# Masked softmax on one core: the first tile's 6-row store is cut into 2 and 4 rows

## The chip, the cores and the metric

The kernel runs on one core of one Trainium2 chip. The metric is the device time of one execution in microseconds. A core has compute engines that work beside each other, each with its own list of instructions: TensorE (PE in the profile), VectorE (DVE), ScalarE (ACT), GpSimd (POOL) and SyncE (SP), which here only issues transfers. They wait for each other by semaphores. Transfers between the chip's memory and the core's on-chip buffer are carried out by 16 transfer (DMA) engines, which take their work from queues: q1 holds what SyncE issues, q0 what GpSimd issues.

## The reference

For each of 16 batches, a softmax along the last axis is taken over the first `length` columns; the columns behind stay zero.

```python
def reference(x, lengths):                    # x: 16 x 8 x 256 x 256 float32
    result = np.zeros_like(x)
    for b in range(batch):
        length = lengths[b]                   # 128 to 255
        masked = x[b, :, :, :length].copy()
        masked = masked - np.max(masked, axis=-1, keepdims=True)
        exp_masked = np.exp(masked)
        result[b, :, :, :length] = exp_masked / np.sum(exp_masked, axis=-1, keepdims=True)
    return result
```

The lengths of the draw are 188, 233, 229, 243, 195, 252, 165, 210, 222, 180, 209, 157, 159, 199, 214 and 248.

## The kernel before

One batch is one tile: 8 x 256 = 2048 rows of 256 columns, laid out as 128 partitions with 16 rows each, so that a partition's share of a tile is 16 KB in one piece in memory. `xt` has 8 slots of a tile; the tile at position n uses slot n modulo 8, and every step works in place. Positions 0, 1 and 2 hold batches 1, 2 and 3, position 3 holds batch 15, positions 4 to 14 the batches of that number, and position 15 holds batch 0 (`batch_of`). "Tile n" below means position n.

The order of work is written out by hand, with a list and semaphores for each engine.

- *Loads.* SyncE loads tile 0 in two halves (L137). GpSimd loads tiles 1 and 2 whole (L185) and all later ones through `pick` (L157), which branches on the batch's length and loads only as many columns as are needed, in steps of 8 from 160 to 240, or all 256; what a load leaves out was zeroed once by `fill` (L180). A load cut off in this way consists of short runs, a full one of 16 KB per partition. In the loop (L193) the load of tile n waits until the load of tile n - 2 has landed (L199) and until the slot's former tile n - 8 has been stored (L200). So about two loads are under way at a time.
- *Compute.* VectorE clips each tile from column 128 on (L241), which puts very low values behind the length; ScalarE takes the exponential row by row with the row's sum (L348), 16 instructions a tile; VectorE then takes the reciprocals of a half tile's 8 sums (L262) and multiplies the half by them (L265). On VectorE the clip of tile b + 1 stands between the two divisions of tile b, except for tile 1.
- *Stores.* SyncE's list (L138 to L148) goes through the tiles and, in each tile, through the pieces that `parts` gives. Each piece waits at L141 for the division of the half that it ends in. The first piece of each tile from tile 2 on waits at L145 until the tile two before has wholly landed. In tile 0 the piece that starts at row 2 also waits at L143 for `s_min` to reach 3, that is, for the clip of tile 1.
- *Semaphores of the stores.* Even and odd tiles have one each, `s_st[0]` and `s_st[1]`. A tile adds 64 in all, whatever its pieces, and both start at 64.
- *End.* After the last tile VectorE looks at the sums (L297 to L308) to see whether the plain path was good enough; if it was, nothing more is computed, and SyncE waits for the last store.

The pieces of a tile are given by `cuts`, in rows per partition:

```python
        if b == 0:
            cuts = [0, 2, half, nt]              # nt = 16, half = 8, quarter = 4
        elif b < 8:
            cuts = [0, half, half + quarter, nt]
```

Tiles 8 to 12 and 15 go out in two halves, 13 and 14 in one piece.

Of the kernel before, what the change touches and what calls it, by code (L numbers as in the profile page):

```python
# [21 lines left out]
def kernel(  # L22
# [12 lines left out]
    nt = rows // P  # L35
    half = nt // 2
    quarter = nt // 4
# [11 lines left out]
    def batch_of(pos):  # L49
        return pos + 1 if pos < ahead else {ahead: 15, 15: 0}.get(pos, pos)  # L50
# [7 lines left out]
    def parts(b):  # L58


        if b == 0:
            cuts = [0, 2, half, nt]
        elif b < 8:
            cuts = [0, half, half + quarter, nt]
        elif b < 13 or b == batch - 1:
            cuts = [0, half, nt]
        else:
            cuts = [0, nt]
        return [slice(i, j) for i, j in zip(cuts, cuts[1:])]
# [30 lines left out]
    with tc.tile_critical(no_gpsimd_drain=True):  # L100
# [34 lines left out]
        for h in range(2):  # L135
            s = slice(h * half, (h + 1) * half)
            nc.sync.dma_start(out=xt[:, 0, s], in_=x_f[batch_of(0), :, s]).then_inc(s_ld[h], 16)  # L137
        for b in range(batch):  # L138
            s_b = s_st[b % 2]
            for s in parts(b):  # L140
                nc.sync.wait_ge(s_out, 2 * b + (s.stop - 1) // half + 1)  # L141
                if b == 0 and s.start == 2:
                    nc.sync.wait_ge(s_min, 3)  # L143
                if b >= 2 and s.start == 0:
                    nc.sync.wait_ge(s_b, 64 * (b // 2 + 1))  # L145
                nc.sync.dma_start(  # L146
                    out=out_f[batch_of(b), :, s, :], in_=xt[:, b % slots, s, :]
                ).then_inc(s_b, 16 * max(1, (s.stop - s.start) // quarter))  # L148
        nc.sync.wait_ge(s_st[0], 64 * (batch // 2 + 1))


# [41 lines left out]
        with nc.Fori(0, batch // 2 - 2, 1, engines=[POOL]) as q:  # L193
            for par in range(2):
                n = 2 * q + (ahead + 1 + par)
                b = n % 15 if par == 1 else n
# [215 lines left out]
```

## Time and profile before

| | |
|---|---|
| median of 3 runs | 155.60 us (155.55, 155.60, 156.01) |
| the profiled execution | 155.76 us, of which 154.0 us from the first to the last instruction |
| busy: VectorE / ScalarE / GpSimd / TensorE | 117.0 / 105.3 / 22.6 / 0.3 us |
| moved | 61.57 MB, mean 400 GB/s |
| read from memory / written to it | 27.98 MB / 33.55 MB |
| transfers issued by SyncE for stores | 38 |

How to read it: the profile shows one execution. "Busy" counts an engine's own work, not its waiting and not the issuing of transfers. The strip of 40 slices gives the busy share of each fortieth of the span in tenths, 9 for 90% or more. A row of the timeline has start and duration in us, engine, line of the kernel, operation and tiles; "SPq" and "POOLq" are the sequencers of SyncE and GpSimd. In the queue view a row gives packets, MB, and the time that the packets took as a share of 16 transfer engines over the stretch looked at. In the table by stretches, each row gives the stretch, its length, the busy time of each engine with the number of its instructions, the granted clock, the busy share of the transfer engines and the GB/s. The chain of waits follows back from the last instruction of a compute engine through what released each step.

### The profile page before, as it was taken

How to read it: one execution, taken by the hardware profiler on the slowest of the kernel's cores; microseconds unless marked ns; L12 is line 12 of the kernel's file. 1: busy time of each engine (PE TensorE's matmuls, PEld its weight loads, DVE VectorE, ACT ScalarE, POOL GpSimd, SP SyncE). 2: the span in 40 equal slices, each digit the busy share in tenths (PEclk: the TensorE clock that was granted, in tenths of full speed). 3: DMA queues.
4: the chain of work that ended last, by engine and by line, in shares of the span. 5: the costliest groups of instructions: out<-in, count | busy, mean ns of one | idle time of the engine just before them, and what ended most of it. 6: DMA issues, size and time to landing. Idle time of an engine off the chain costs nothing.

```text
span 154.0 us, 1308 instructions
## 1 busy us (share of the span) xinstructions
PE 0.3 (0%) x2; PEld 0.2 (0%) x2; DVE 117.0 (76%) x91; ACT 105.3 (68%) x514; POOL 22.6 (15%) x30
## 2 busy tenths in 40 slices
PE   0000000000000000000000000000000000000000
PEld 0000000000000000000000000000000000000000
DVE  1349899988969696969698796969696566596820
ACT  3097799579595959596886949595959709639300
POOL 4893000102030200202020030211020000000000
DMA  4999999999999999999999999999999999999992
GB/s 102 424 449 430 420 358 387 425 432 427 410 400 386 422 408 422 411 412 417 400 419 414 408 418 403 415 418 412 414 425 418 424 408 419 420 445 434 415 424 100
DMA packets 10501, 61.57 MB, mean 400 GB/s; under 512 B 882, under 2 KB 994, under 8 KB 6914
## 3 DMA queue, kind: packets, MB, share of 16 engines
q1 hardware_dynamic: 5760, 35.65, 56.5%
q0 software_dynamic: 4736, 25.89, 41.7%
q14 instruction: 3, 0.02, 0.0%
q10 hardware_dynamic: 2, 0.00, 0.0%
HBM read 27.98 MB, written 33.55 MB: 400 GB/s over the span
## 4 chain that ended last, share of the span: by engine, by line
DMA 65%; DVE 17%; ACT 5%; issue 5%; ACTq 1%; POOLq 1%; POOL 1%; SPq 1%; PE 0%
DMA xt<-in_x_dram 43%; DMA out_dram<-xt 21%; DVE xt L265 9%; DVE xt L241 6%; ACT xt L348 5%; ACTq L348 1%; POOL xt L180 1%; DMA word<-in_lengths_dram 1%; DVE inv_sum L262 1%; SPq L146 1%; DVE ends L297 0%; POOLq L127 0%; POOLq L162 0%; POOLq L157 0%; DVE bad L300 0%
## 5 line engine op out<-in xcount | busy, mean ns | idle before, releaser
L348 ACT ACTIVATE xt<-xt (+1 forms) x256 | 102.4, 401 | 36.7 <-DVE xt L241 36.7
L265 DVE TENSOR_TENSOR xt<-xt,inv_sum 128x2048 f32<-128x2048 f32 x32 | 73.3, 2291 | 1.1
L348 ACT ACTIVATION_READ_ACCUMULATOR xt<-xt (+1 forms) x256 | 47.8, 187 | 0.0
L241 DVE SCALAR_TENSOR_TENSOR xt<-down,len_s,xt 128x2048 f32<-128x2048 f32 (+1 forms) x17 | 37.8, 2222 | 10.9 <-DMA xt<-in_x_dram 10.7
L157 POOL DMA_DIRECT2D xt<-in_x_dram x13 | 13.8, 1060 | 90.3 <-DMA out_dram<-xt 56.6
L262 DVE RECIPROCAL inv_sum<-row_sum 128x8 f32<-128x8 f32 x32 | 6.3, 198 | 16.0 <-ACT xt L348 16.0
L180 POOL MEMSET xt<- 128x1536 f32 x5 | 6.7, 1399 | 1.1 <-DVE len_s L232 1.1
L341 ACT ACT_TABLE_LOAD x1 | 1.3, 1283 | 1.6 <-SPq L100 1.6
L224 DVE TENSOR_SCALAR down<-iota_i 128x256 f32<-128x256 int32 x1 | 0.3, 299 | 1.6 <-POOL iota_i L170 1.6
L185 POOL DMA_DIRECT2D xt<-in_x_dram x2 | 1.2, 620 | 0.0
L297 DVE TENSOR_REDUCE ends<-row_sum 128x1 f32<-128x256 f32 x2 | 0.7, 408 | 0.0
L211 PE MATMUL count<-bad,ones_c 128*1 128x3 bf16 x1 | 0.2, 165 | 144.5 <-DVE bad L300 144.5
L229 DVE CAST len_b<-word 1x16 bf16<-1x16 int32 x1 | 0.2, 163 | 0.4 <-DMA word<-in_lengths_dram 0.4
L232 DVE TENSOR_SCALAR len_s<-len_f 128x16 f32<-128x16 f32 x1 | 0.2, 175 | 0.4 <-PE len_f L209 0.4
L170 POOL IOTA iota_i<- 128x256 int32 x1 | 0.3, 331 | 0.6 <-SPq L100 0.6
L308 DVE TENSOR_REDUCE redo<-count 1x1 f32<-1x3 f32 x1 | 0.1, 149 | 0.3 <-PE count L211 0.3
L300 DVE TENSOR_SCALAR bad<-ends 128x1 bf16<-128x1 f32 x3 | 0.3, 150 | 0.0
L211 PEld LDWEIGHTS count<-bad,ones_c 128*1 128x1 bf16 x1 | 0.1, 79 | 144.6 <-DVE bad L300 144.6
L176 POOL MEMSET seed<- 1x1 f32 x2 | 0.2, 226 | 0.0
L341 ACT ACTIVATE warm<-const-float32-0.0 128x1 f32<-128x1 f32 x1 | 0.2, 202 | 0.0
L173 POOL MEMSET ones<- 1x128 bf16 x1 | 0.2, 194 | 0.0
L209 PE MATMUL len_f<-len_b,ones 1*128 1x16 bf16 x1 | 0.2, 167 | 2.6 <-DVE len_b L229 2.6
(8 smaller groups left out, 0.8 us busy)
## 6 DMA issues: line engine op xcount, KB each, us to landing
out_dram<-xt SPq DMA_DIRECT2D x20, 1024.0 KB
xt<-in_x_dram POOLq DMA_DIRECT2D x4, 2048.0 KB, 14.7
out_dram<-xt SPq DMA_DIRECT2D x14, 512.0 KB
xt<-in_x_dram POOLq DMA_DIRECT2D x3, 1728.0 KB, 16.9
out_dram<-xt SPq DMA_DIRECT2D x2, 2048.0 KB
xt<-in_x_dram POOLq DMA_DIRECT2D x2, 1600.0 KB, 18.9
xt<-in_x_dram POOLq DMA_DIRECT2D x2, 1280.0 KB, 13.9
xt<-in_x_dram SPq DMA_DIRECT2D x2, 1024.0 KB, 6.6
```

The costliest lines, as they stand in the source:

```text
L146: nc.sync.dma_start(out=out_f[batch_of(b), :, s, :], in_=xt[:, b % slots, s, :]).then_inc(s_b, 16 * max(1, (s.stop - s.start) // quarter))
L157: nc.gpsimd.dma_start(out=xt[:, slot, :, :w], in_=x_n[:, b, :, :w]).then_inc(s_sw[par], 16)
L170: nc.gpsimd.iota(iota_i, pattern=[[1, seq_k]], base=0, channel_multiplier=0).then_inc(s_iota, 1)
L180: nc.gpsimd.memset(xt[:, b, :, low:], 0.0).then_inc(s_fill, 1)
L185: nc.gpsimd.dma_start(out=xt[:, b], in_=x_f[batch_of(b)]).then_inc(s_ld[b + 1], 16)
L211: nc.tensor.matmul(count, lhsT=ones_c, rhs=bad, start=True, stop=True).then_inc(s_count, 1)
L241: return nc.vector.scalar_tensor_tensor(out=t, in0=down[:, None, lo:hi].to_broadcast([P, s.stop - s.start, hi - lo]), scalar=len_s[:, batc ...
L262: step(nc.vector.reciprocal(out=inv_sum[:, b, s], in_=row_sum[:, b, s]))
L265: nc.vector.tensor_tensor(out=t, in0=t, in1=inv_sum[:, b, s, None].to_broadcast([P, half, seq_k]), op=ALU.mult,).then_inc(s_out, 1)
L297: step(nc.vector.tensor_reduce(out=ends[:, k : k + 1], in_=values, op=op, axis=AX))
L341: nc.scalar.activation(out=warm, in_=nc.const_aps.tensor(0.0, (P, 1), F32), func=EXP)
L348: ins = nc.scalar.activation(out=e, in_=e, func=EXP, accum_out=sum_h[:, i, j])
```

## The change

For the first tile, the piece from row 2 to row 8 is cut at row 4. The tile goes out as rows 0 to 2, 2 to 4, 4 to 8 and 8 to 16 of each partition: 256, 256, 512 and 1024 KB instead of 256, 768 and 1024 KB. Its four pieces add 16 each to `s_st[0]`, 64 in all as before; before, the three added 16, 16 and 32. All other tiles have the same pieces and the same increments as before. The waits at L141, L143 and L145 are unchanged; the one at L143 now stands ahead of the piece of rows 2 to 4.

```diff
         if b == 0:
-            cuts = [0, 2, half, nt]
+            cuts = [0, 2, quarter, half, nt]
         elif b < 8:
             cuts = [0, half, half + quarter, nt]
...
                 nc.sync.dma_start(
                     out=out_f[batch_of(b), :, s, :], in_=xt[:, b % slots, s, :]
-                ).then_inc(s_b, 16 * max(1, (s.stop - s.start) // quarter))
+                ).then_inc(s_b, 16 * (1 if b == 0 else (s.stop - s.start) // quarter))
```

In the order of instructions only SyncE's list changes: it has one transfer more, the others' lists are the same.

## The prediction

> **What bounds the kernel now.** I read the page first: the span, the busy shares, the strip of 40 slices, the queues. Then the chain of waits, SyncE's waits at the end, and a table by stretches.
>
> ```profile
> span 154.0 us, 1308 instructions
> PE 0.3 (0%) x2; PEld 0.2 (0%) x2; DVE 117.0 (76%) x91; ACT 105.3 (68%) x514; POOL 22.6 (15%) x30
> DMA  4999999999999999999999999999999999999992
> DMA packets 10501, 61.57 MB, mean 400 GB/s; under 512 B 882, under 2 KB 994, under 8 KB 6914
> q1 hardware_dynamic: 5760, 35.65, 56.5%
> q0 software_dynamic: 4736, 25.89, 41.7%
> ```
>
> No compute engine is over 76%, while the transfer engines stand at 9 from the second slice to the second last. Queue q1 holds the first tile's two loads and all 38 stores, each of 128 data packets and 16 tiny ones: 40 x 144 = 5760. Queue q0 holds the other loads.
>
> The chain of waits seems to say something else:
>
> ```profile
> 134.56 2.36 DVE xt L241
> 143.94 2.29 DVE xt L265
> 147.53 0.15 DVE redo L308
> ```
>
> It follows the last load through the last tile's compute, but it stops at the last engine instruction, at 147.7. SyncE, whose sequencer the chain does not end on, then still waits for stores:
>
> ```profile
> SPq L407 <- DMA out_dram<-xt: 3.4, 1, 3.4
> ```
>
> So the end is when the last store lands. Whether that is set by the chain (the last store is issued late) or by the transfers (the stores ahead of it are still going out) is told by the stretches. Behind the clock column stand the transfer engines' busy share and GB/s:
>
> ```profile
> 2.00:134.50 132.50, 0.17 (x1) 0.10 (x1) 105.82 (x76) 98.48 (x482) 21.68 (x20) 1.00 1.02 411
> 134.50:146.30 11.80, 0.00 (x0) 0.00 (x0) 9.81 (x8) 6.50 (x32) 0.00 (x0) 1.00 1.01 431
> 146.30:151.00 4.70, 0.17 (x1) 0.08 (x1) 1.09 (x7) 0.00 (x0) 0.00 (x0) 1.00 0.96 406
> 151.00:154.00 3.00, 0.00 (x0) 0.00 (x0) 0.00 (x0) 0.00 (x0) 0.00 (x0) 1.00 0.05 22
> 146.26 0.37 SPq L146 DMA_DIRECT2D out_dram<-xt  x1
> ```
>
> The last row is the last store's issue. After it 4.70 x 406 + 3.0 x 22 kB/us = 1.97 MB still goes out, and that store is 1.05 MB (128 x 8 KB). So 0.92 MB lies ahead of it, some 2.2 us at 431 GB/s: the transfers set the end. Idle before 151 is about 4% of 4.70 us, 0.19 us. The last 1.8 us belong to a few transfer engines that run behind the rest (share 0.05).
>
> **The change part by part.** The first tile's 6-row store becomes one of 2 and one of 4 rows. Bytes, loads and compute stay. Three things remain to be costed.
>
> *Packet time.* Each of 16 transfer engines carries 8 of a store's 128 packets. Prices come from the queue view: share x 16 x window / packets. The pairs below are of the windows 17.4 to 20.4 us, 24.6 to 26.6, 28 to 31, and 38 to 40, in which q1's packets hold 2, 6, 8 and 4 KB.
>
> ```profile
> q0 software_dynamic: 85, 1.13, 88.3%
> q1 hardware_dynamic: 72, 0.15, 12.6%
> ...
> q1 hardware_dynamic: 78, 0.48, 57.0%
> q0 software_dynamic: 77, 0.37, 44.7%
> ...
> q1 hardware_dynamic: 96, 0.79, 62.6%
> q0 software_dynamic: 96, 0.46, 38.2%
> ...
> q0 software_dynamic: 43, 0.70, 82.1%
> q1 hardware_dynamic: 42, 0.17, 20.9%
> ```
>
> So 2 KB take 0.126 x 48 / 72 = 84 ns, 6 KB 234 ns, 8 KB 313 ns, 4 KB 159 ns; of the loads, a 4.8 KB packet takes 191 ns and a 16 KB packet 611 ns. Removed per engine: 8 x 234 = 1.87 us. Added: 8 x (84 + 159) = 1.94 us. Net +0.07 us; one more tiny packet for the semaphore I put at 0.01. Bounds: zero if time went by bytes alone, 8 x 84 = 0.67 us if the 4 KB packet still took what 6 KB took. The 159 ns row denies the latter, so I take +0.08.
>
> *SyncE's extra issue.* It costs about 0.37 us (the row above).
>
> ```profile
> 13.69 5.32 SPq L146 DMA_DIRECT2D out_dram<-xt  x3
> 13.77 2.35 DVE L241 SCALAR_TENSOR_TENSOR xt<-down,len_s,xt 128x2048 f32<-128x2048 f32 x1
> 16.27 2.29 DVE L265 TENSOR_TENSOR xt<-xt,inv_sum 128x2048 f32<-128x2048 f32 x1
> ```
>
> The three issues of tile 0 lie between 13.69 and 19.01. The 8-row one waits for the division that ends at 16.27 + 2.29 = 18.56. The second waits at L143 for the clip of tile 1, which ends at 13.77 + 2.35 = 16.12. Another issue of 0.37 us fits into the 2.4 us between. Price 0; without that cover 0.37 us of SyncE's time, still not of the transfers'. The 4-row piece adds no wait: its two conditions were met by the piece before it.
>
> *Who goes first.* While both queues hold work they alternate packet by packet: 96 to 96 from 28 to 31 us. Hence the 6-row store let 8 load packets per engine pass and the 2+4 pair lets 16 pass. From about 24 us, when the first piece and the 16 KB loads are done, q0 holds tile 4's load: 1.6 MB in packets of 4.8 KB (0.46 MB / 96), so 21.3 per engine. Before, these pass 8 x 6 KB and 13.3 x 8 KB of stores: 21.3 x 0.191 + 8 x 0.234 + 13.3 x 0.313 = 10.1 us. After, 8 x 2 KB, 8 x 4 KB and 5.3 x 8 KB: 4.07 + 0.67 + 1.27 + 1.66 = 7.7 us. The load lands about 2.4 us sooner. Tile 0's stores were through after 16 pairs, 1.87 + 2.50 + 3.06 = 7.4 us; now after 24 pairs, the last 2.7 of them beside 16 KB packets: 0.67 + 1.27 + 2.50 + 4.07 + 1.65 = 10.2 us, 2.7 us later. Who waits for that:
>
> ```profile
> 32.44 0.37 SPq L146 DMA_DIRECT2D out_dram<-xt  x1
> 26.95 2.29 DVE L265 TENSOR_TENSOR xt<-xt,inv_sum 128x2048 f32<-128x2048 f32 x1
> 27.43 0.54 POOL L157 DMA_DIRECT2D xt<-in_x_dram  x1 [12.11 <-issue]
> 37.66 1.17 POOL L157 DMA_DIRECT2D xt<-in_x_dram  x1 [9.69 <-issue]
> 52.74 1.15 POOL L157 DMA_DIRECT2D xt<-in_x_dram  x1 [7.80 <-DMA out_dram<-xt]
> ```
>
> SyncE issues tile 2's stores at 32.44 although their first half was divided by 29.24: L145 holds them until tile 0 is out. That goes to about 35.1, with tile 1's 2 MB still queued, at 0.42 MB/us some 5 us of work at full speed, so q1 does not run dry. The load into tile 0's slot is the one at 52.74, the sixth on L157; it has over 17 us to spare. And the load at 37.66 waits for tile 4's load (L199): it can go some 2 us sooner, and each later one likewise, two loads apart. Loads gain a lead, stores pay for it, and the sum of transfer work is the same. At the end the lead makes the last store's issue earlier, behind more backlog: worth at most the 0.19 us of idle above. That idle lies mostly on engines that finish early, so I take 0.
>
> Sum: 155.76 us was the profiled execution (154.0 of span and 1.76 around it), plus 0.08 makes 155.84. The median of the runs is 155.60, 0.16 below that execution, so the forecast is 155.7.
>
> **A rule that speaks against it.** The Trainium skill, "DMA: Bandwidth & Descriptors", section "Anatomy of one DMA", gives a transfer a fixed cost of about 2.0 us and advises fewer, larger ones. If that fell on the path once more, an estimate by the page would be 157.7 us. This trace does not agree that it adds up: 411 GB/s at a share of 1.02 over 132.5 us leaves no room for a fixed 2 us in each of some 50 transfers; the page itself lays most of it to the completion.
>
> **The rivals.**
> *Slower: the slow reads last longer.* One stretch loses speed at a full share:
>
> ```profile
> 17.00:20.00 3.00, 0.00 (x0) 0.00 (x0) 1.98 (x2) 3.00 (x17) 0.00 (x0) 1.00 1.03 433
> 20.00:24.00 4.00, 0.00 (x0) 0.00 (x0) 3.97 (x3) 4.00 (x22) 0.00 (x0) 1.00 0.98 337
> ```
>
> Both hold 2 KB stores beside 16 KB loads. If writes of 2 KB pieces at a stride of 16 KB disturb the reads, 8 more pairs of 2 KB and 4.8 KB, 8 x 0.275 = 2.2 us, would run at 337 instead of 433 GB/s: 2.2 x (433/337 - 1) = 0.6 us, 156.3. It decides if those pairs come out 15% or more slow. Against it: from 17 to 20 the same mix ran at 433.
>
> *Slower: a fixed price per transfer.* The first load is issued at 1.13 us and nothing moves before 2; 0.9 us of such dead time on the ring would give 156.6. It needs an empty ring, and at 16.6 us q0 is full.
>
> *Faster: the end is at a knee.* The last store has 2.2 us of backlog ahead of it, and a store needs time before its first packet: at least the 0.9 us just named, and the first store, issued at 13.69, moves nothing until 17.3:
>
> ```profile
> DMA packets 93, 1.52 MB, mean 421 GB/s; under 512 B 0, under 2 KB 0, under 8 KB 0
> q0 software_dynamic: 92, 1.51, 100.3%
> ```
>
> (13.7 to 17.3 us: q1 has no packet; load packets that the engines had already taken up may be part of this.) Where the last load comes a microsecond later than in this execution, the transfers idle before the last store, and a lead of some 2 us removes that. The runs reach from 155.55 to 156.01; if the median holds half a microsecond of it, 155.1. Against it: this execution has nearly no such idle and is not among the fastest.
>
> *The change does not do what it says:* if the alternation were by whole transfers, loads would gain little. The time stays 155.7; it is within the forecast's case.
>
> **How the numbers follow.** The forecast within 0.3% (0.47 us, about what a measurement of this kernel can tell from no change): 0.60. Knee: 0.20, faster. Slow reads: 0.15, and the fixed price 0.05, slower. The range 155.0 to 156.5 takes in the knee's 155.1 and the slow reads' 156.3 with 0.1 to 0.2 around them and leaves out the fixed price. The forecast's own range is 155.4 to 156.0.
>
> **What would show it.** q1 with 41 x 144 = 5904 packets and unchanged 35.65 MB; four issues of tile 0 instead of three; tile 2's first store issued near 35 instead of 32.4, the load at 37.66 near 35.5; the last load's clip 1 to 4 us before 134.56; share 1.0 up to 151 and the same end. Wrong: a share below 0.95 before 146 (a queue ran dry), GB/s near 340 beyond 24 us (slow reads), or an end over 0.5 us sooner, which the backlog does not allow.

## The result, and the profile after

The changed kernel took 155.22 us in the median (154.85 to 155.37, 13 runs), the kernel before on the same chip 155.55 us (154.99 to 156.01, 13 runs): a ratio of 0.9975 with an interval of 0.9966 to 0.9985. A second measurement, described below, gave 0.9969 (0.9959 to 0.9979). So the change takes away about a third to half of a microsecond, at the edge of the 0.3% that the prediction called the least that can be told. The forecast was 0.08 us more, 155.7. The time lies inside the whole range of 155.0 to 156.5, but below the forecast's own part of it, 155.4 to 156.0, and the direction is another.

The page of the changed kernel, the lines that answer to those of before:

```profile
span 153.0 us, 1309 instructions
DMA packets 10645, 61.57 MB, mean 402 GB/s; under 512 B 898, under 2 KB 1010, under 8 KB 7058
q1 hardware_dynamic: 5904, 35.65, 56.6%
q0 software_dynamic: 4736, 25.89, 41.8%
```

q1 has the 144 packets more that one more store brings, and the same megabytes. But the packets' time together fell: 98.4% of 153.0 us is 150.6 us for each transfer engine, against 98.2% of 154.0, 151.2 us. More packets for the same bytes took less time.

The table by stretches and SyncE's wait at the end, of the changed kernel (the last two columns are the transfer engines' busy share and GB/s):

```profile
2.00:134.50 132.50, 0.17 (x1) 0.10 (x1) 110.43 (x79) 101.02 (x495) 21.71 (x20) 1.00 1.02 413
134.50:146.30 11.80, 0.17 (x1) 0.08 (x1) 6.15 (x11) 3.99 (x21) 0.00 (x0) 1.00 1.01 431
146.30:151.00 4.70, 0.00 (x0) 0.00 (x0) 0.00 (x0) 0.00 (x0) 0.00 (x0) 1.00 0.91 382
151.00:153.00 2.00, 0.00 (x0) 0.00 (x0) 0.00 (x0) 0.00 (x0) 0.00 (x0) 1.00 0.01 4
SPq L407 <- DMA out_dram<-xt: 4.2, 1, 4.2
```

The transfers are busy to the end as before, only that the end comes sooner: after 151 us hardly anything is left. Timeline rows of the changed kernel show the steps that were foretold:

```profile
16.05 2.71 SPq L146 DMA_DIRECT2D out_dram<-xt  x3
34.15 1.17 POOL L157 DMA_DIRECT2D xt<-in_x_dram  x1 [7.60 <-DMA out_dram<-xt]
35.15 1.88 SPq L146 DMA_DIRECT2D out_dram<-xt  x3
129.39 2.35 DVE L241 SCALAR_TENSOR_TENSOR xt<-down,len_s,xt 128x2048 f32<-128x2048 f32 x1
142.07 0.87 SPq L146 DMA_DIRECT2D out_dram<-xt  x2
```

Three issues of tile 0 follow the first one between 16.05 and 18.76. Tile 2's stores go at 35.15 instead of 32.44, the load of tile 6 at 34.15 instead of 37.66. The last clip starts at 129.39 instead of 134.56, and the last two stores are issued together from 142.07, 3 us and more ahead of 146.26.

So where did the time go? Look at the stretch in which the first profile ran at 337 GB/s. The queue view from 21.0 to 23.2 us, first of the kernel before, then of the changed one; q0 holds the 16 KB loads of tile 3, q1 the 2 KB stores:

```profile
q0 software_dynamic: 40, 0.66, 98.7%
q1 hardware_dynamic: 39, 0.07, 8.2%
...
q0 software_dynamic: 49, 0.80, 91.0%
q1 hardware_dynamic: 47, 0.08, 9.1%
```

A 16 KB load packet took 0.987 x 16 x 2.2 us / 40 = 869 ns before and 654 ns after; undisturbed it takes 611. That is 40 x 258 / 16 = 0.65 us lost by each transfer engine before, and 0.13 us after. This is no accident of one execution: a second profile of the kernel before has 879 ns there, and two kernels of the experiments below that begin like it have 834 and 839; two further profiles of the changed kernel have 635 and 653 ns, and one that begins like it 651. The changed kernel pays part of it back a little later (23.6 to 26.6 us):

```profile
q0 software_dynamic: 162, 0.77, 72.5%
q1 hardware_dynamic: 160, 0.37, 31.0%
```

Here a load packet of 4.8 KB takes 0.725 x 48 us / 162 = 215 ns instead of 191, 0.24 us for each transfer engine. In the three other profiles that begin like the changed kernel it takes 199 to 210 ns, 0.1 to 0.2 us.

### The profile page after: what moved, and what is told of

It reads as the page before. It is cut to its first block, busy times and chain, and to the rows that moved or that the text cites. A ratio compares the mean times of both kernels' runs of the same rounds, so it can differ in the third digit from the quotient of the medians.

```text
span 153.0 us, 1309 instructions
## 1 busy us (share of the span) xinstructions
PE 0.3 (0%) x2; PEld 0.2 (0%) x2; DVE 116.9 (76%) x91; ACT 105.4 (69%) x514; POOL 22.6 (15%) x30
## 3 DMA queue, kind: packets, MB, share of 16 engines
q1 hardware_dynamic: 5904, 35.65, 56.6%
## 4 chain that ended last, share of the span: by engine, by line
DVE 48%; ACT 17%; issue 11%; DMA 10%; ACTq 6%; POOL 1%; POOLq 0%; PE 0%; SPq 0%
DVE xt L265 24%; DVE xt L241 21%; ACT xt L348 17%; DMA xt<-in_x_dram 9%; ACTq L348 5%; DVE inv_sum L262 2%; POOL xt L180 1%; DMA word<-in_lengths_dram 1%; ACTq L354 1%; DVE ends L297 0%; POOLq L127 0%; DVE bad L300 0%; DVE len_s L232 0%; PE len_f L209 0%; PE count L211 0%
```

## The experiments

The three theories at first: K, the knee at the end (the prediction's faster rival); R, the slow reads at 20 to 24 us; N, chance in how far the slowest transfer engine runs behind. All runs of one group were taken beside the kernel before on one chip; the ratio is to that.

**The kernel before, a second profile.** No edit.

> The kernel before, unchanged, for a second profile of it. Theory K (knee): in some executions of before the transfer engines stand idle for some tenths of a us ahead of the last store, because the last load came late; the change takes that away. Then this profile shows, for its own time, as much idle between 143 and 151 us as it lies above 155.1 us. Theory R (slow reads): before loses its time at 20 to 24 us, where the first profile had 337 GB/s and that of the changed kernel 392. Then this profile again shows about 340 GB/s there. Theory N: neither, the two profiles differ by how far the slowest transfer engine runs behind, which varies from one execution to the next; then 20 to 24 us lies anywhere between 340 and 430 GB/s and the tail has no idle.

It took 155.41 us, with 353 GB/s from 20 to 24 us (337 in the first profile). The slow stretch is there again, as R said. A second profile of the changed kernel, for which 380 to 400 GB/s were expected there, had 393 (155.14 us). N does not explain this: the profiles of the two kernels don't overlap in this stretch.

**A shorter end, in both kernels.**

```diff
-            clip(b, s, mid, seq_k).then_inc(s_min, 1)
+            clip(b, s, seq_k - 8 if b == batch - 1 else mid, seq_k).then_inc(s_min, 1)
```

> The kernel before, with the clip of the last tile cut to its last 8 columns (columns 128 to 247 of batch 0 are left unmasked). Everything up to the last load is the same; only the chain from the last load to the last store's issue gets some 2.1 us shorter. K: the last store is no longer late in any execution, so the median falls by about 0.3 us to 155.2 and the spread shrinks to that of the changed kernel. R and N: no change, 155.55, since nothing before 134 us is touched and the end is set by the transfers.

> The changed kernel with the same cut of the last tile's clip (columns 128 to 247 of batch 0 are left unmasked). K, R and N: no gain over the changed kernel, 155.2, because its last store is issued 3.8 us sooner than before and has backlog enough. If this is clearly below 155.2, the tail of the changed kernel still has idle, and all three are incomplete.

In the kernel before: 155.50 us, ratio 0.9997 (0.9983 to 1.0011). In the changed one: 155.11 us, 0.9973 (0.9960 to 0.9986) of the kernel before, no more than the change alone gives. In the timeline and the table of the shortened kernel before, the last two stores go out from 143.09 instead of ending with one at 146.26, and nothing is won by it:

```profile
143.09 0.87 SPq L146 DMA_DIRECT2D out_dram<-xt  x2
146.30:151.00 4.70, 0.00 (x0) 0.00 (x0) 0.00 (x0) 0.00 (x0) 0.00 (x0) 1.00 0.96 406
```

The last row is the same as in the kernel before, 0.96 and 406 GB/s. K is out: the backlog in front of the last store sufficed.

**No 2 KB packets at all.**

```diff
-            cuts = [0, 2, half, nt]
+            cuts = [0, half, nt]
```

> The kernel before without its 2-row piece: tile 0 goes out in two halves of 8 rows. No 2 KB packets run beside the 16 KB loads; the loads of tiles 3 and 4 are passed by 8 KB packets instead and land about 2.4 us later (8 x 0.23 us for the first, the rest for the second). K: the last load is as much later and the knee is left far behind, 1.5 to 2.4 us slower, 157.0 to 158.0, with idle transfers ahead of the last store. R: the disturbed reads go, 0.3 to 0.7 us faster, 154.9 to 155.2. N: the same, 155.5.

155.35 us, 0.9989 (0.9975 to 1.0003): neither K's loss nor R's full gain, and not told apart from no change. Its last store is issued at 146.39, hardly later than the 146.26 of before, so the loads were not delayed as expected and this run tests K less than was meant. Its trace says why (below, with its counterpart): the slow stretch did not go, it moved ahead of the first 8 KB store packet, which stands at 17.6 us. So it is not the 2 KB writes that disturb the reads. From here on the theory was F: a store with larger packets costs when it joins. Its rival M: the gain comes from the number of pieces and small packets.

**The second piece with 4 KB packets.** From the changed kernel:

```diff
-            cuts = [0, 2, quarter, half, nt]
+            cuts = [0, 2, half - 2, half, nt]
```

> Tile 0 in pieces of 2, 4, 2 and 8 rows: the same number of pieces and of store packets as the changed kernel, and the same lead of the loads, but the second piece has 4 KB packets. Theory F: when a store with larger packets joins 16 KB loads, the engines take in its packets before any of them goes out, and the loads slow down in the 2 to 3 us before; the larger the joining packet, the more is lost. Before (6 KB joining) lost 0.82 us per engine on the 16 KB loads, the changed kernel (2 KB joining) 0.27. F: about 0.5 us lost here, time 155.3 to 155.45, between the two. Theory M: the gain comes from the alternation with more and smaller store packets, wherever they stand. M: as the changed kernel, 155.2, and 0.27 us lost.

155.39 us, 0.9984 (0.9973 to 0.9996): between the two, as F said, but the interval also holds the changed kernel's 0.9975, so the time does not decide against M. The load packets do better: from 21.0 to 23.2 us they took 1.010 x 35.2 us / 45 = 790 ns, between 654 and 869. This is one profile:

```profile
q0 software_dynamic: 45, 0.74, 101.0%
```

**Stores held back until the 16 KB loads are nearly out.** At the second piece in the kernel before and in the changed one, and at the first of two halves:

```diff
-                    nc.sync.wait_ge(s_min, 3)
+                    nc.sync.wait_ge(s_min, 4)
...
-            cuts = [0, 2, half, nt]
+            cuts = [0, half, nt]
...
-                if b == 0 and s.start == 2:
-                    nc.sync.wait_ge(s_min, 3)
+                if b == 0 and s.start == 0:
+                    nc.sync.wait_ge(s_min, 4)
```

> The kernel before (2, 6, 8 rows) with the 6-row piece held until the clip of tile 2 is done (s_min at 4 instead of 3), at about 22.0 instead of 16.2 us. The 6 KB packets then join when the 16 KB loads are nearly out, at about 24 us. F: the loss on the 16 KB loads falls from 0.82 to 0.3 us or less, and the time to 155.1 to 155.25, as in the changed kernel, though the packets are those of before. M: no gain, 155.55. If a queue ran dry at 24 us it would be slower than before by the length of the gap.

> The changed kernel (2, 2, 4, 8) with the second piece held in the same way to about 22.0 us. F: little is left to take away, 155.1 to 155.2. M: 155.2.

> Tile 0 in two halves of 8 rows, the first of them held until the clip of tile 2 is done (about 22.0 instead of 13.7 us). No store runs beside the 16 KB loads of tiles 2 and 3, which should be out by 23.5 us. F: next to nothing is lost on the 16 KB loads (0.9 us with the same pieces and no hold), so 154.6 to 154.9, faster than both kernels. M: fewer and larger packets than before and no small ones, so 155.4 to 155.6. If the loads run out before the store's first packet, a gap shows near 24 us and the time rises by it.

Measured: 155.47 us, 0.9982 (0.9971 to 0.9992), for the kernel before; 155.34 us, 0.9989 (0.9968 to 1.0010), for the changed one; 155.40 us, 0.9981 (0.9970 to 0.9993), for the halves. F expected 155.1 to 155.25, 155.1 to 155.2 and 154.6 to 154.9 and was wrong in all three: without 16 KB loads beside it, the joining store costs as well (332 GB/s from 24 to 25.9 us in the first). The halves lie where M put them, and the gain of 0.2% in the first is the only one that M did not expect, so these times hardly speak against M. The clearest pair is that of two halves, without and with the hold. Stretches 15.5 to 17.5 and 23 to 25 us, first of the kernel without the hold, then of the one with it; behind each pair of rows, q0 from 15.5 to 17.5 us in the same kernel:

```profile
15.50:17.50 2.00, 0.00 (x0) 0.00 (x0) 1.97 (x3) 1.18 (x6) 0.00 (x0) 1.00 1.00 307
23.00:25.00 2.00, 0.00 (x0) 0.00 (x0) 2.00 (x1) 2.00 (x11) 0.00 (x0) 1.00 1.05 422
q0 software_dynamic: 37, 0.61, 98.4%
...
15.50:17.50 2.00, 0.00 (x0) 0.00 (x0) 1.97 (x3) 1.18 (x6) 0.00 (x0) 1.00 1.04 430
23.00:25.00 2.00, 0.00 (x0) 0.00 (x0) 1.97 (x3) 2.00 (x11) 0.00 (x0) 1.00 1.05 308
q0 software_dynamic: 53, 0.85, 103.0%
```

The compute engines do the same from 15.5 to 17.5. The store was issued at 13.6 us in the one kernel and at 21.7 in the other, its first packet stands at 17.6 and at 25.0 us, and the slow stretch goes with it: 307 and 430 GB/s early, 422 and 308 late, always at a full share. In the slow stretches q1 has not one packet yet. Transfers run slow ahead of the store's first packet, while its issue is done and its data has not begun to leave. That is theory J, what is left of F: the packet size of the store that joins decides, and the loads beside it don't. (Every piece has 128 packets, so larger packets also mean more bytes in the piece; no run separates the two.)

**The first piece cut instead of the second.** From the changed kernel:

```diff
-            cuts = [0, 2, quarter, half, nt]
+            cuts = [0, 1, 2, half, nt]
```

> Tile 0 in pieces of 1, 1, 6 and 8 rows: one piece and eight store packets per engine more than before, as in the changed kernel, but it is the first piece that is cut, and 6 KB packets follow on 1 KB ones. Theory J (what is left of F): transfers run slow for 2 to 3 us ahead of the first packet of a store whose packets are larger than those before it, whatever loads run beside it; the second piece's size decides (16 KB loads at 20 to 24 us: 6 KB 0.65 us per engine lost, 4 KB 0.5, 2 KB 0.15 and some 0.25 more on the next load). J: a loss of 0.65 us or more as before, time 155.5 to 155.65. Theory M (number of pieces and packets): 155.2, as the changed kernel.

155.43 us, 0.9992 (0.9981 to 1.0002): not told apart from before, although it has as many pieces and packets as the changed kernel. It is a little below the 155.5 to 155.65 that J gave, and the 16 KB loads were not slowed (611 ns each from 21 us on): the slow stretch, 309 GB/s, is at 22.8 to 25.0 us, when the loads' packets are already short. The first 6 KB packet stands at 25.2 us. A load packet, 4.6 KB in the mean, took 0.824 x 35.2 us / 122 = 238 ns:

```profile
q0 software_dynamic: 122, 0.56, 82.4%
q1 hardware_dynamic: 123, 0.12, 15.2%
```

**More small pieces.** From the changed kernel, first with 2, 2, 2, 2, 8 rows, then with 2, 2, 2, 2, 4, 4 (all semaphore counts of the stores doubled, so that five or six pieces fit into a tile's sum):

```diff
-            cuts = [0, 2, quarter, half, nt]
+            cuts = [0, 2, quarter, 6, half, nt]
...
+            cuts = [0, 2, quarter, 6, half, half + quarter, nt]
```

> Tile 0 in pieces of 2, 2, 2, 2 and 8 rows; the semaphores of the stores count in units twice as large, which costs no instruction. J: no larger packets join until the 8-row piece, when the loads' packets are small; the loss on the 16 KB loads stays at about 0.15 us and that of the step to 4 KB (0.25 us) is put off, against 8 x (2 x 84 - 159) ns = 0.07 us of packet time more. 155.0 to 155.2. M: more pieces again, 154.9 to 155.1. If the 8-row piece brings a loss of 0.65 us behind 24 us: 155.5.

> The changed kernel again, beside the two below on one chip. J and M: 0.9975 of before as in its first measurement, 155.2.

> Pieces of 2, 2, 2, 2 and 8 rows again. J: the loss between 15 and 28 us was 0.32 us per engine in its first profile, that of the changed kernel 0.33 and 0.53 in two; with 0.07 us more packet time it should stand within 0.15 us of the changed kernel, on either side. M: below it by as much again as the changed kernel is below before, 0.3 us.

> Pieces of 2, 2, 2, 2, 4 and 4 rows: also the 8-row piece is cut, so that packets grow from 2 to 4 KB while tile 5's 16 KB loads are under way, and 8 KB come with tile 1. J: little is left to save, and 8 x (2 x 159 - 313) ns = 0.04 us is added: within 0.15 us of the run above. M: lower again by 0.2 to 0.3 us.

The five pieces gave 155.08 us, 0.9965 (0.9953 to 0.9978), and, on one chip with the others, 155.09 us, 0.9965 (0.9952 to 0.9978). There the changed kernel had 155.17 us, 0.9969 (0.9959 to 0.9979), and the six pieces 155.47 us, 0.9989 (0.9977 to 1.0002). Five pieces and the changed kernel can't be told apart, and a further cut loses: M, by which each further cut gains, is out. That the six pieces lie 0.4 us above the five is more than J allowed (0.15). Their rate from 20 to 28 us does not show it; but their profiled execution took 155.15 us, 0.32 below their median, so this trace can't show where the others lost their time. The stretch from 20 to 28 us in the order before, 1-1-6-8, changed (two profiles), 2-2-2-2-8, 2-2-2-2-4-4:

```profile
20.00:28.00 8.00, 0.00 (x0) 0.00 (x0) 7.90 (x7) 8.00 (x42) 0.54 (x1) 1.00 0.99 378
20.00:28.00 8.00, 0.00 (x0) 0.00 (x0) 7.90 (x7) 8.00 (x41) 0.54 (x1) 1.00 0.99 376
20.00:28.00 8.00, 0.00 (x0) 0.00 (x0) 7.90 (x7) 8.00 (x41) 0.54 (x1) 1.00 1.00 389
20.00:28.00 8.00, 0.00 (x0) 0.00 (x0) 7.90 (x7) 8.00 (x42) 0.54 (x1) 1.00 0.98 394
20.00:28.00 8.00, 0.00 (x0) 0.00 (x0) 7.90 (x7) 8.00 (x41) 0.54 (x1) 1.00 1.01 402
20.00:28.00 8.00, 0.00 (x0) 0.00 (x0) 7.90 (x7) 8.00 (x41) 0.54 (x1) 1.00 1.00 401
```

Shares are alike and compute is the same; only the rate differs, 376 to 378 where 6 KB packets follow on smaller ones and 389 to 402 where 2 KB do. The kernel with 2, 4, 2 and 8 rows, not in the table, has 378 as well, so this rate alone does not put it between the two.

**Joining three times more.** In the kernel before, the first store of tiles 3, 5 and 7 also waits for the tile ahead of it:

```diff
                     nc.sync.wait_ge(s_b, 64 * (b // 2 + 1))
+                    if b in (3, 5, 7):
+                        nc.sync.wait_ge(s_st[(b - 1) % 2], 64 * ((b - 1) // 2 + 2))
```

> The kernel before, with the first store of tiles 3, 5 and 7 held until the tile before it has wholly landed, so that the store queue runs empty three times and three 8 KB stores join anew. J: each joining costs about 0.65 us per engine at a busy share near 1.0 and a rate near 300 GB/s for 2 us, so 2 us in all, 157.0 to 158.0. If joining costs nothing (the slow stretch belongs to 20 to 24 us alone): 155.5 to 155.9 as long as the loads fill the gaps; where they don't, the share falls below 0.95 there and the time rises by that idle alone.

157.49 us, 1.0119 (1.0104 to 1.0133), the 2 us that J gave, but not for J's reason alone. Tile 3's stores are issued from 55.1 us. The stretches 53 to 57 and 57.5 to 59 us, and q0 in each:

```profile
53.00:57.00 4.00, 0.00 (x0) 0.00 (x0) 3.97 (x4) 2.11 (x11) 0.45 (x1) 1.00 1.02 374
57.50:59.00 1.50, 0.00 (x0) 0.00 (x0) 1.50 (x1) 1.50 (x9) 0.62 (x1) 1.00 1.06 298
...
q0 software_dynamic: 360, 1.48, 100.7%
...
q0 software_dynamic: 96, 0.43, 103.3%
```

From 57.5 us on a 4.5 KB load packet takes 1.033 x 24 us / 96 = 258 ns, against 1.007 x 64 / 360 = 179 ns just before, of about 4.1 KB in the mean. That is the joining, far from 20 to 24 us; only two store packets stand in this stretch. But already from 53 to 57 us, with loads alone, the rate is 374 GB/s, where the kernel before moves 8 KB stores beside them at 412. An estimate from these two stretches: the loads alone lose 4 x (1 - 374 / 412) = 0.37 us, the joining 1.5 x (1 - 298 / 412) = 0.41 us. So short load packets with hardly a store beside them lose about as much, and the three joinings were not separated from that: the agreement with J's 2 us is in part luck.

## Why the prediction was right or wrong

- *What bounds the kernel: right.* The chain of waits ends at the last engine instruction and does not set the time. A last store issued almost 3 us sooner changed nothing. One reading was off: the last 1.8 us of the span don't belong to transfer engines that run behind. The last data packet ends at 152.3 us, and nothing is moved from there to the span's end at 154.0 (151.4 and 153.0 in the changed kernel). No term of the sum rests on it.
- *SyncE's issue, the counts, who goes first: right in kind.* 5904 packets; load of tile 6 earlier by 3.5 us (2 foretold); tile 2's stores at 35.15 (35.1 foretold); last clip 5.2 us earlier (1 to 4 foretold). The lead of the loads came out larger than foretold, and the hit on 35.1 is in part luck, since it was worked out with packet times that did not hold at 21 to 27 us. As said, the lead is worth nothing.
- *Packet time: probably right, and small.* 0.08 us; no run isolates it.
- *"Loads gain a lead, stores pay for it, and the sum of transfer work is the same": wrong, and this is the step that failed.* The sum of transfer work fell, because a packet's time is no constant. I took 84, 159, 234 and 313 ns from calm stretches and left out the 0.65 us that an engine lost from 21.0 to 23.2 us before the 6 KB packets came. With the measured terms: -0.65 + 0.13 + 0.24 + 0.08 = -0.20 us, and up to -0.36 with the smallest payback of the other profiles, 0.08. The medians differ by 0.33 and by 0.48 us in the two measurements, and the first interval runs from -0.23 to -0.53. So most of the gain is accounted for, and 0.1 to 0.3 us of it is open if the larger payback holds. The two profiled executions differ by 0.9 us (155.76 and 154.85), which is the "end over 0.5 us sooner" that the prediction had named as a sign of being wrong. Part of that is chance: the first profile of the changed kernel already moved 410 GB/s from 2 to 15 us, where the kernels are still the same, against 402 in the kernel before and 403 in its own second profile.
- *The slow reads, taken for a slower rival: the right stretch, the wrong cause and sign.* It was put down to 2 KB writes and was to grow by 0.6 us with more of them. The halves without any 2 KB packet showed it too, at 307 GB/s, and ahead of their first write. I used its rate as a price and did not ask what came right behind it: the first 6 KB packet stands at its end, at 23.3 us.
- *The knee: wrong.* The kernel before with a shorter end says so.
- *The rule from the Trainium skill* ("DMA: Bandwidth & Descriptors", "Anatomy of one DMA": about 2.0 us fixed per transfer): no run agrees that it adds up here. The section gives the figure for transfers issued by GpSimd, while the store that was cut is SyncE's, and the advice to use fewer, larger transfers stands in another section of the page. One store more came out 0.3 to 0.5 us faster than before, two more about as much, and three more 0.2 us, not told apart from no change; none came near 2 us slower. Most of that cost lies in the completion, says the page; here other transfers go on meanwhile, at a busy share of 1.02.

What is shown: the slow stretch stands ahead of a store with larger packets and moves with its issue, and its load packets got shorter with the second piece's packet size (6, 4, 2 KB: 869, 790, 654 ns). The medians go the same way (155.55, 155.39, 155.22), though the middle one's interval also holds the changed kernel's ratio. Not shown is that the loss grows beyond 6 KB: in the halves without the hold, where 8 KB join, a 16 KB load packet took 0.984 x 32 us / 37 = 851 ns from 15.5 to 17.5 us, a loss of 37 x (851 - 611) ns / 16 = 0.56 us, about that of 6 KB and not more. What is argued only: that the transfer engines take in the coming store's data in that time, in step with the loads, and can put nothing out for it. The trace has no row for that. Open remain the six pieces' 155.47 us, and how much the step from 2 to 8 KB costs: from 27 to 29 us, ahead of its first 8 KB packet, the 2-4-2-8 kernel has 414 GB/s and the two profiles of 2-2-2-2-8 have 364 and 404, against 434 in the kernel before, where 8 KB packets were already going out.

## What to carry to other kernels

When the transfer engines are full from end to end, do not take a packet's price from a calm stretch alone: look for stretches with a full share and a low rate, and ask what store or load is about to begin behind each. Let stores join a running stream of loads with small packets first and grow from there; here 2, 2, 4, 8 rows and 2, 2, 2, 2, 8 rows did about equally well, 0.3% ahead of 2, 6, 8. Cutting further or cutting the first piece gained 0.1%, not told apart from nothing, and holding the stores back 0.1 to 0.2%. A lead of the loads by 5 us at the end was worth nothing, since the last store already had about 2 us of backlog ahead of it.

## What the runs showed of the hardware

Three things were not expected. In this kernel an issued store slowed the transfers for some 2 us before its own first packet: 307 instead of 430 GB/s, at a share of 1.00. Loads in short packets (4.1 KB in the mean) with hardly a store packet beside them ran at 374 GB/s, slower than the mixed stream at 412. And a share of 1.0 in the table by stretches is no sign of full speed: it was 1.00 at 307 GB/s and 1.04 at 430.
